# A decoder layer on one core: stick-breaking weights by a VectorE scan along the keys and TensorE transposes, tokens in reverse order, and banded attention's bias and row maximum in one VectorE instruction

## The chip, the cores and the metric

The kernel runs on one core of a Trainium2 chip. Time is device time in microseconds (us) of one execution of the whole program, and lower is better. The engines are named as in the profile: PE is TensorE (matrix products; PEld is its weight load, which overlaps), DVE is VectorE, ACT is ScalarE, POOL is GpSimd and SP is SyncE, which here only issues transfers. Three runs of the kernel before gave 802.22 to 802.78 us.

## The reference

One decoder layer on 512 tokens of width 1024, in float32. After an RMS norm, one wide projection feeds three mixers, each with its own sigmoid gate: banded attention (8 query heads, 2 key heads, window 128, a bias by distance, a sink), stick-breaking attention (8 heads of 64), and attention over 256 memory tokens (4 heads of 128). Then a projection, a second norm and a SwiGLU layer. The parts that the change touches:

```python
# stick-breaking, for every query t (rows) and key s (columns), z = q.k / 8
causal = key < query
log_1m  = where(causal, log_sigmoid(-z), 0)
between = reverse_cumsum(log_1m) - log_1m          # over keys between s and t
a       = where(causal, exp(log_sigmoid(z) + between), 0)
out     = a @ v
# banded attention, 128 queries against 256 keys
scores = where(in_window, scores + bias, -inf)
m = max(max(scores), sink);  p = exp(scores - m)
w = p / (sum(p) + exp(sink - m))
```

So the weight of key s is sigmoid(z) times the product of 1 - sigmoid(z) over the keys that lie between it and the query.

## The kernel before, in words

Everything is computed with tokens or features on the 128 partitions. A float32 product is made of three products of parts: `split` (L134) writes a rounded high part on ACT (L136) and the rest on DVE (L137), and `mm3` (L166) multiplies high by high, high by low and low by high (L168 to L170).

The work is laid out in one Python program, from which a scheduler makes the order on each engine: it goes by program order as priority, by when it expects an instruction's inputs to be there, and by the buffers that are free. `after` (L187) adds order edges that cost no wait. On the chip each engine then works through its list in order and waits where an input is late. Two helpers shape the program order:

- `Stream` (L33) holds the dense projections (weight load by SP, split, products) in a queue of units, and `run(us)` emits units worth about `us` of PE time. The attention code calls it between its own stages, so that PE has projections to work on while ACT and DVE prepare the next attention products. A generator `yield 7.0` in `sb_head` is such a request for 7.0 us.
- `table` (L199) loads an ACT function table and pins every later function call behind it; Exp and Ln share one table, Sigmoid has another.

`sb_head` (L838 on) runs once for each of 8 heads, in `SEG`ments of the causal triangle packed in three PSUM tiles of 512, 384 and 384 columns (the last one holds the two smallest blocks). Scores are transposed, keys on the partitions: eight products and three mask products into `z`. ACT and DVE form softplus(z) by Abs, Exp, Ln (L869 and the two calls after it) and a DVE combination (L872), which is then split into `sh` and `sl` (L877, L878). After the filler of 7.0 us PE adds the sum over keys into the same `z` by products with a triangle of -1 (`ntri_r`) and blocks of -1 (`none_r`, `none`), 14 records in all; ACT takes Exp, and the result is the weight tile that the value product `ysb` reads, once for every two heads.

`swa_pair` (L913) does banded attention for two heads at a time: scores with queries on the partitions, bias added on DVE (L933 to L935) into a tile whose unused first block POOL fills (L932), row maxima by `tensor_reduce` (L943), Exp on ACT with a running sum, a scaling on DVE (L955), seven transposes through PE (L966), copies, and the value product `ysw`.

[...] The gates of stick-breaking are projected between the heads; their Sigmoid runs in one block when all heads are done (`sigmoids`, L325), between two table loads. The values of both mixers lie in `v_all`, written at L347.

Of the kernel before, what the change touches and what calls it, by code (L numbers as in the profile page):

```python
# [10 lines left out]
F32 = mybir.dt.float32  # L11
# [94 lines left out]
def tile_kernel(ctx, tc, a):  # L106
# [251 lines left out]

    def vcols(t, lo):
        return v_all[:, t * 640 + lo : t * 640 + lo + 64]  # L360
# [24 lines left out]
    def mem_keys(i):  # L385
        def gen(hi, lo):
            if i % 2 == 0:
                st[("mk", i // 2)] = ck(f"mk{i}")
            t = st[("mk", i // 2)][:, (i % 2) * M : (i % 2 + 1) * M]
            ps = dps(f"pmk{i}")  # L390
            for k in range(KC):
                mm3(ps[:, :M], cols((hi, lo), k * P, P), mu[k], k == 0, k == KC - 1)
                yield 0.325
            nc.vector.tensor_tensor(t, ps[:, :M], st["mrb"][:, :], op=ALU.mult)
            if i % 2 == 1:
                st[("mks", i // 2)] = parts(f"mks{i // 2}", st[("mk", i // 2)])

        return gen

    def mem_vals(q):  # L400
        def gen(hi, lo):
            if q == 0:
                st["pmv"] = [dps(f"pmv{t}") for t in range(2)]
            for i in range(2):
                k = 2 * q + i
                for t in range(2):
                    x = (mu[k][0][:, t * P : (t + 1) * P], mu[k][1][:, t * P : (t + 1) * P])
                    mm3(st["pmv"][t][:, :], x, cols((hi, lo), i * 512, 512), k == 0, k == KC - 1)
                    yield 0.65
                    if k == KC - 1:  # L410
                        vt = ck(f"mv{t}")
                        nc.vector.tensor_scalar(
                            vt[:, :], st["pmv"][t][:, :], st["mrs"][:, t : t + 1], None, op0=ALU.mult
                        )
                        st[("mvs", t)] = parts(f"mvs{t}", vt)

        return gen
# [358 lines left out]
    ntri = const("ntri", [P, P])  # L776
# [5 lines left out]
    sinks = cst.tile([P, 8], F32, name="sinks")  # L782
    nc.sync.dma_start(sinks[:, :], a["sinks"].to_broadcast([P, 8]))
    ntri_r = cst.tile([P, P], F32R, name="ntri_r")
    nc.gpsimd.tensor_copy(ntri_r[:, :], ntri[:, :])
    none = cst.tile([P, P], F32, name="none")
    nc.gpsimd.memset(none[:, :], -1.0)
    nc.gpsimd.tensor_scalar(g_neg[:, :], g_pre, -1.0, None, op0=ALU.mult)
    none_r = cst.tile([P, P], F32R, name="none_r")
    nc.gpsimd.tensor_copy(none_r[:, :], none[:, :])  # L790

# [46 lines left out]
    def sb_head(h):  # L838
        c = h // 2
        ks, qs, ql = (st[(x, c, h % 2)] for x in ("kbs", "qbs", "qbl"))  # L840
        z = [aps(f"z{h}{i}") for i in range(3)]

        def seg(ts, j):
            i, o, n = SEG[j]
            return ts[i][:, o : o + n]

        for j in range(4):
            i, o, n = SEG[j]
            kj = slice(j * P, (j + 1) * P)
            if j < 3:  # L850
                out, qh, qlo = z[i][:, o : o + n], qs[:, j * P :], ql[:, j * P :]
            else:

                out = z[i][:, o : o + 2 * n]
                qh = qs[:, j * P :].unsqueeze(1).to_broadcast([P, 2, P])
                qlo = ql[:, j * P :].unsqueeze(1).to_broadcast([P, 2, P])
            mm(out, ks[:, kj], qh, j < 3, False)
            mm(out, ks[:, kj], qlo, False, False)

        for i in range(2):  # L860
            mm(z[i][:, :P], identb[:, :], negm[:, :], False, False)
        blocks23 = z[2][:, :].rearrange("p (b n) -> p b n", b=4)[:, 0:4:2, :]
        mm(blocks23, identb[:, :], negm[:, :].unsqueeze(1).to_broadcast([P, 2, P]), False, False)
        e = [ck(f"e{h}{i}") for i in range(3)]
        sh = [ck(f"sh{h}{i}", F32R) for i in range(3)]
        sl = [ck(f"sl{h}{i}", F32R) for i in range(3)]
        for i in range(3):
            x, n = e[i][:, : W[i]], W[i]
            nc.scalar.activation(x, z[i][:, :n], AF.Abs)  # L869
            fn(x, x, AF.Exp, scale=-1.0)  # L870
            st["chain"] = fn(x, x, AF.Ln, bias=1.0)
            nc.vector.scalar_tensor_tensor(x, z[i][:, :n], 0.0, x, op0=ALU.max, op1=ALU.add)  # L872
            if i == 2:

                nc.vector.tensor_tensor(e[i][:, 384:], e[i][:, 128:256], e[i][:, 256:384], op=ALU.add)
                x, n = e[i][:, :], 512
            nc.vector.tensor_copy(sh[i][:, :n], x)  # L877
            nc.vector.tensor_tensor(sl[i][:, :n], x, sh[i][:, :n].bitcast(F32), op=ALU.subtract)  # L878
        yield 7.0

        def both(t):

            return t[2][:, :].rearrange("p (b n) -> p b n", b=4)[:, 0:4:3, :]


        for j in range(3):
            for t in (sh, sl):
                mm(z[j][:, : W[j]], ntri_r[:, :], t[j][:, : W[j]], False, j == 2 and t is sl)
        for t in (sh, sl):
            mm(z[0][:, 128:], none_r[:, :], seg(t, 1), False, False)  # L890
        for t in (sh, sl):
            mm(z[0][:, 256:], none_r[:, :], both(t), False, t is sl)
            mm(z[1][:, 128:384], none_r[:, :], both(t), False, t is sl)
        mm(z[2][:, 128:256], none[:, :], seg(e, 3), False, True)
        for i in range(3):
            fn(e[i][:, : W[i]], z[i][:, : W[i]], AF.Exp)
        yield 3.0 if h % 2 == 0 else 4.0
        if h % 2 == 0:
            st["even"] = e
            return  # L900


        ys = aps(f"ysb{c}")
        for j in (3, 2, 1, 0):
            for i, x in ((1, e), (0, st["even"])):
                mm(ys[64 * i : 64 * i + 64, j * P :], vcols(j, 128 + (2 * c + i) * 64), seg(x, j), j == 3, j == 0)
        pair_out(SB, c, ys)


    def blocks(t, n):  # L910
        return t[n // 2][:, (n % 2) * 256 : (n % 2) * 256 + 256]

    def swa_pair(c, bias):  # L913
        hs = (c, c + 4)
        s, w, pt, pts = {}, {}, {}, {}
        for i, h in enumerate(hs):
            qs, ks, kl = st[("qas", c, i)], st[("kas", 0, i)], st[("kal", 0, i)]
            s[h] = [aps(f"s{h}{i}") for i in range(2)]
            for n in (1, 0, 2, 3):
                q = slice(n * P, (n + 1) * P)  # L920
                if n == 0:
                    kh = ks[:, :P].unsqueeze(1).to_broadcast([P, 2, P])
                    klo = kl[:, :P].unsqueeze(1).to_broadcast([P, 2, P])
                else:
                    keys = slice((n - 1) * P, (n + 1) * P)
                    kh, klo = ks[:, keys], kl[:, keys]
                mm(blocks(s[h], n), qs[:, q], kh, n in (1, 2), False)
                mm(blocks(s[h], n), qs[:, q], klo, False, True)
        for h in hs:
            b = bias[h // 2][:, (h % 2) * 256 : (h % 2) * 256 + 256]  # L930
            w[h] = [ck(f"w{h}{i}") for i in range(2)]
            nc.gpsimd.memset(w[h][0][:, :P], NEG)  # L932
            nc.vector.tensor_tensor(w[h][0][:, P:256], s[h][0][:, P:256], b[:, P:256], op=ALU.add)  # L933
            nc.vector.tensor_tensor(w[h][0][:, 256:], s[h][0][:, 256:], b, op=ALU.add)
            nc.vector.tensor_tensor(  # L935
                w[h][1][:, :].rearrange("p (n k) -> p n k", n=2),
                s[h][1][:, :].rearrange("p (n k) -> p n k", n=2),
                b.unsqueeze(1).to_broadcast([P, 2, 256]),
                op=ALU.add,
            )  # L940
            nm, den, es = (small(f"{x}{h}") for x in ("nm", "den", "es"))
            for i in range(2):
                nc.vector.tensor_reduce(  # L943
                    nm[:, 2 * i : 2 * i + 2], w[h][i][:, :].rearrange("p (n k) -> p n k", n=2), axis=AX.X, op=ALU.max
                )
            nc.vector.tensor_scalar(nm, nm, sinks[:, h : h + 1], -1.0, op0=ALU.max, op1=ALU.mult)
            fn(es, nm, AF.Exp, bias=sinks[:, h : h + 1])
            for n in range(NT):
                x = blocks(w[h], n)
# [3 lines left out]
            for n in range(NT):  # L953
                x = blocks(w[h], n)
                nc.vector.tensor_scalar(x, x, den[:, n : n + 1], None, op0=ALU.mult)  # L955
        yield 10.0
        for h in hs:

            pt[h] = [aps(f"pt{h}{i}") for i in range(2)]
            for n in range(NT):  # L960
                for e in range(2):
                    j = n - 1 + e
                    if j < 0:
                        continue
# [3 lines left out]
            nc.scalar.copy(pts[h][0][:, :], pt[h][0][:, :])  # L968
            nc.vector.tensor_copy(pts[h][1][:, :384], pt[h][1][:, :384])
        yield 2.0  # L970
        ys = aps(f"ysw{c}")
        for j in range(NT):
            n = 256 if j < 3 else P
            for i, h in enumerate(hs):
                mm(ys[64 * i : 64 * i + 64, j * P : j * P + n], vcols(j, i * 64), blocks(pts[h], j)[:, :n], j == 0, j == 3)
# [43 lines left out]
    bias = band_bias()  # L1019
    for h in range(8):  # L1020
# [4 lines left out]
    table("sigmoid_and_others")  # L1025
    sigmoids(SB)
# [544 lines left out]
def _constants():  # L1571
# [3 lines left out]
    for k in range(128):  # L1575
        oh[b[k], 255 - k] = 1.0
    wm = np.full((P, 384), NEG, np.float32)
    wm[:, 128:256] = 0.0
    return {
        "ident": np.eye(P, dtype=np.float32),  # L1580
        "ntri": -(i[:, None] >= i[None, :]).astype(np.float32),
# [6 lines left out]
def _layout(i):  # L1588
# [5 lines left out]
    x, mem = i["x"][0], i["mem"][0]  # L1594
# [60 lines left out]
```

## Time and profile before

| What | Value |
|---|---|
| median of 3 runs | 802.58 us |
| profiled execution, first to last instruction | 801.9 us |
| PE / DVE / ACT / POOL busy | 791.9 / 608.0 / 474.8 / 105.2 us |
| granted PE clock | 0.998 |
| DMA | 123.43 MB, mean 154 GB/s |
| stick-breaking heads | about 80 to 213 us |
| banded attention | about 215 to 290 us |

A row of groups in the profile gives line, engine, operation, written and read tiles, shape, count, then busy time in total, mean duration of one in ns, and the engine's idle time before them with what ended it. A row of the timeline gives start, length, engine, line, operation, tiles, shape and count. PE records overlap (the next one starts before the modelled end of the last one), so a PE instruction's price is the distance from its start to the start of the next one, not its duration.

### The profile page before, as it was taken

The page shows a single profiled execution, that of the slowest core. Times are in us where ns is not written, and L with a number is a line of the kernel's source. Part 1 is how long each engine was busy: PE and PEld are TensorE (multiplying, and loading weights), DVE is VectorE, ACT ScalarE, POOL GpSimd, SP SyncE. Part 2 cuts the span into 40 slices and gives each one's busy share as a digit, 9 for nine tenths or more (in the row PEclk, how much of TensorE's full clock was granted, in tenths as well). Part 3 has the DMA queues.
Part 4 walks back from the last instruction along what each step waited for, and adds up shares of the span by engine and source line. Part 5 has one row for each costly group of instructions (what it writes and reads, how often), then busy time and mean ns, then how long its engine had stood idle before and what let it go on. Part 6 is the DMA issues. An engine that isn't in the chain of part 4 may idle for free.

```text
span 801.9 us, 12466 instructions
## 1 busy us (share of the span) xinstructions
PE 791.9 (99%) x4694; PEld 695.8 (87%) x4694; DVE 608.0 (76%) x957; ACT 474.8 (59%) x847; POOL 105.2 (13%) x131
## 2 busy tenths in 40 slices
PE   9999999999999999999999999999999999999996
PEld 6899888778788888888888899999999999888785
DVE  6895878656578876766876679867676777898797
ACT  7562766546776587557823466655544444666573
POOL 1203300000020120002062100100100000215200
PEclk9999999999999999999999999999999999999999
DMA  8444535221572478339869707987777762949802
GB/s 298 134 133 124 202 106 148 64 74 57 171 167 58 79 137 212 73 77 242 290 203 289 133 5 184 266 237 184 184 182 184 183 158 64 220 106 241 182 0 105
DMA packets 42876, 123.43 MB, mean 154 GB/s; under 512 B 5056, under 2 KB 6768, under 8 KB 42816
## 3 DMA queue, kind: packets, MB, share of 16 engines
q1 hardware_dynamic: 30912, 86.32, 33.6%
q0 software_dynamic: 11472, 35.93, 24.3%
q8 instruction: 36, 0.59, 0.3%
q10 hardware_dynamic: 432, 0.39, 0.1%
q14 instruction: 24, 0.20, 0.1%
HBM read 116.85 MB, written 3.67 MB: 150 GB/s over the span
## 4 chain that ended last, share of the span: by engine, by line
PE 88%; DVE 5%; DMA 3%; issue 2%; ACT 1%; POOL 1%; DVEq 0%; POOLq 0%; ACTq 0%
PE gx L168 5%; PE gx L170 5%; PE gx L169 5%; PE z L180 4%; DMA bp<-in_w_dn 3%; PE gy L170 3%; PE gy L168 3%; PE gy L169 3%; PE br L168 3%; PE br L169 3%; PE br L170 3%; PE mx L170 2%; PE mx L169 2%; PE mx L168 2%; PE g L168 2%
## 5 line engine op out<-in xcount | busy, mean ns | idle before, releaser
L136 ACT CAST hi<-gw 128x1024 fp32r<-128x1024 f32 x77 | 79.9, 1048 | 83.5 <-DVE gw L1231 39.9
L137 DVE TENSOR_TENSOR lo<-gw,hi 128x1024 fp32r<-128x1024 f32 x77 | 93.8, 1227 | 32.4 <-ACT hi L136 32.4
L137 DVE TENSOR_TENSOR lo<-raw,hi 128x1024 fp32r<-128x1024 f32 (+2 forms) x76 | 91.8, 1208 | 33.8 <-ACT hi L136 33.4
L136 ACT CAST hi<-raw 128x1024 fp32r<-128x1024 f32 (+2 forms) x76 | 78.4, 1037 | 44.7 <-PE pv L170 10.7
L1213 POOL DMA_DIRECT2D gw<-in_w_gu x27 | 23.3, 920 | 196.5 <-DMA gw<-in_w_gu 71.4
L136 ACT CAST hi<-r 128x1024 fp32r<-128x1024 f32 (+1 forms) x24 | 23.5, 981 | 19.8 <-PE y L170 5.3
L168 PE MATMUL x<-hi,lh 128*128 128x512 f32 x88 | 34.4, 390 | 0.3 <-ACT lh L136 0.3
L169 PE MATMUL x<-lo,lh 128*128 128x512 f32 x88 | 34.3, 389 | 0.0
L170 PE MATMUL x<-hi,ll 128*128 128x512 f32 x88 | 34.2, 390 | 0.0
L137 DVE TENSOR_TENSOR lo<-r,hi 128x1024 fp32r<-128x1024 f32 (+1 forms) x24 | 27.2, 1132 | 3.6 <-ACT hi L136 3.5
L137 DVE TENSOR_TENSOR lo<-bp,hi 128x512 fp32r<-128x512 f32 x33 | 22.7, 719 | 7.0 <-ACT hi L136 6.8
L456 POOL DMA_DIRECT2D raw<-in_w_g x16 | 13.9, 868 | 106.7 <-DVE lo L137 92.9
L193 ACT ACTIVATE e<-e 128x384 f32<-128x384 f32 (+1 forms) x48 | 26.9, 561 | 1.5
L136 ACT CAST hi<-bp 128x512 fp32r<-128x512 f32 x33 | 19.4, 620 | 14.1 <-DMA bp<-in_w_dn 5.0
L872 DVE SCALAR_TENSOR_TENSOR e<-z,e 128x384 f32<-128x384 f32 (+1 forms) x24 | 14.3, 597 | 15.7 <-ACT e L193 15.7
L168 PE MATMUL g<-uh,hi 128*128 128x512 f32 x64 | 25.4, 398 | 0.0
L170 PE MATMUL g<-uh,lo 128*128 128x512 f32 x64 | 25.3, 396 | 0.0
L168 PE MATMUL gx<-B11h,hi 128*128 128x256 f32 x88 | 25.1, 285 | 0.2 <-ACT B11h L1142 0.2
L168 PE MATMUL gx<-T4h,hi 128*128 128x256 f32 x88 | 25.1, 285 | 0.0
L169 PE MATMUL g<-ul,hi 128*128 128x512 f32 x64 | 25.0, 391 | 0.0
L170 PE MATMUL gy<-N22h,lo 128*128 128x256 f32 x88 | 25.0, 284 | 0.0
L168 PE MATMUL gy<-N22h,hi 128*128 128x256 f32 x88 | 25.0, 284 | 0.0
(792 smaller groups left out, 2831.5 us busy)
## 6 DMA issues: line engine op xcount, KB each, us to landing
gw<-in_w_gu SPq DMA_DIRECT2D x57, 512.0 KB, 4.9
gw<-in_w_gu POOLq DMA_DIRECT2D x27, 512.0 KB, 7.3
raw<-in_w_p SPq DMA_DIRECT2D x22, 512.0 KB, 3.7
raw<-in_w_g POOLq DMA_DIRECT2D x16, 512.0 KB, 6.1
raw<-in_w_g SPq DMA_DIRECT2D x12, 512.0 KB, 3.6
bp<-in_w_dn SPq DMA_DIRECT2D x22, 256.0 KB, 11.2
r<-in_w_dn POOLq DMA_DIRECT2D x10, 512.0 KB, 9.2
raw<-in_w_brt SPq DMA_DIRECT2D x8, 512.0 KB, 4.4
```

The lines of the kernel that those rows point to most:

```text
L136: ins = nc.scalar.copy(hi, raw)
L137: lows = nc.vector.tensor_tensor(lo, raw, hi.bitcast(F32), op=ALU.subtract)
L168: one = nc.tensor.matmul(out, lh, rh, start=start, stop=False, skip_group_check=True)
L169: nc.tensor.matmul(out, lh, rl, start=False, stop=False, skip_group_check=True)
L170: return one, nc.tensor.matmul(out, ll, rh, start=False, stop=stop, skip_group_check=True)
L180: return nc.tensor.matmul(out, l, r, start=start, stop=stop, skip_group_check=True)
L193: ins = nc.scalar.activation(*args, **kw)
L456: nc.gpsimd.dma_start(t[:, :], src, accum_op=ALU.add)
L872: nc.vector.scalar_tensor_tensor(x, z[i][:, :n], 0.0, x, op0=ALU.max, op1=ALU.add)
L1213: nc.gpsimd.dma_start(gw[(n, key)][:, :], g_src(n, i, j), accum_op=ALU.add)
```

## The change

Stick-breaking now has queries on the partitions and keys along the columns, and the host hands over the tokens in reverse, so that the keys behind a query stand to its right, nearest first. ACT writes sigmoid(z) and sigmoid(-z); a DVE scan along the columns computes state = (1 - b)·state + b, the running sum of the weights. The tile is then turned by ten PE transposes of 128 x 128 a head, copied out of PSUM by ACT, and multiplied with differences of neighbouring values instead of the values (summation by parts). For these, eight transfers on SP copy `v_all` shifted by one token, and four DVE subtractions follow the first head's scans. The three triangle and block products and their splits are gone.

Because the heads now use Sigmoid, the table is switched before the heads, once the memory's norm (`mrs`) is there, and the gates' Sigmoids run one by one as each gate is projected. Banded attention uses one `tensor_tensor_reduce` for each block (bias added, maximum with the sink folded in) in place of add, fill and reduce, with the band on the right side, and ACT and DVE swap their two copies. Two evacuations of the memory keys and values get high priority, and some constants go.

```diff
+    def next_values():
+        st["vnext"] = [ck(f"vnext{t}") for t in range(NT)]
+        for t, x in enumerate(st["vnext"]):
+            if t == NT - 1:
+                nc.vector.memset(x[96:, :], 0.0)
+            else:
+                nc.sync.dma_start(x[P - 1 :, :], own_values(t + 1)[:1, :])
+            nc.sync.dma_start(x[: P - 1, :], own_values(t)[1:, :])
+
+    def value_steps():
+        for t, x in enumerate(st.pop("vnext")):
+            after(nc.vector.tensor_tensor(own_values(t), own_values(t), x[:, :], op=ALU.subtract), st["scan"])
...
-            nc.vector.tensor_tensor(t, ps[:, :M], st["mrb"][:, :], op=ALU.mult)
+            with tc.high_priority():
+                nc.vector.tensor_tensor(t, ps[:, :M], st["mrb"][:, :], op=ALU.mult)
...
-            mm(out, ks[:, kj], qh, j < 3, False)
-            mm(out, ks[:, kj], qlo, False, False)
+            mm(out, qs[:, q], keys, r < 3, False)
+            mm(out, ql[:, q], keys, False, False)
...
+        w = [ck(f"bw{h}{i}") for i in range(3)]
+        rest = [ck(f"br{h}{i}") for i in range(3)]
         for i in range(3):
-            x, n = e[i][:, : W[i]], W[i]
-            nc.scalar.activation(x, z[i][:, :n], AF.Abs)
-            fn(x, x, AF.Exp, scale=-1.0)
-            st["chain"] = fn(x, x, AF.Ln, bias=1.0)
-            nc.vector.scalar_tensor_tensor(x, z[i][:, :n], 0.0, x, op0=ALU.max, op1=ALU.add)
-            if i == 2:
-                nc.vector.tensor_tensor(e[i][:, 384:], e[i][:, 128:256], e[i][:, 256:384], op=ALU.add)
-                x, n = e[i][:, :], 512
-            nc.vector.tensor_copy(sh[i][:, :n], x)
-            nc.vector.tensor_tensor(sl[i][:, :n], x, sh[i][:, :n].bitcast(F32), op=ALU.subtract)
-        yield 7.0
+            n = W[i]
+            fn(rest[i][:, :n], z[i][:, :n], AF.Sigmoid, scale=-1.0)
+            st["chain"] = fn(w[i][:, :n], z[i][:, :n], AF.Sigmoid)
+        for i, o, n in SEG:
+            x, r = w[i][:, o : o + n], rest[i][:, o : o + n]
+            st["scan"] = nc.vector.tensor_tensor_scan(x, r, x, 0.0, op0=ALU.mult, op1=ALU.add)
+        yield 7.5
...
-        for j in range(3):
-            for t in (sh, sl):
-                mm(z[j][:, : W[j]], ntri_r[:, :], t[j][:, : W[j]], False, j == 2 and t is sl)
-        for t in (sh, sl):
-            mm(z[0][:, 128:], none_r[:, :], seg(t, 1), False, False)
-        for t in (sh, sl):
-            mm(z[0][:, 256:], none_r[:, :], both(t), False, t is sl)
-            mm(z[1][:, 128:384], none_r[:, :], both(t), False, t is sl)
-        mm(z[2][:, 128:256], none[:, :], seg(e, 3), False, True)
-        for i in range(3):
-            fn(e[i][:, : W[i]], z[i][:, : W[i]], AF.Exp)
+        pt = [aps(f"zt{h}{i}") for i in range(3)]
+        at = [ck(f"at{h}{i}") for i in range(3)]
+        KEY = [(2, 256), (2, 0), (1, 0), (0, 0)]
+        for r in range(NT):
+            i, o, _ = SEG[r]
+            for j in range(r, NT):
+                t, base_col = KEY[j]
+                nc.tensor.transpose(
                    pt[t][:, base_col + r * P : base_col + (r + 1) * P],
                    w[i][:, o + (j - r) * P : o + (j - r + 1) * P],
                    ident[:, :],
                )
+        nc.scalar.copy(at[0][:, :], pt[0][:, :])
+        nc.scalar.copy(at[1][:, :384], pt[1][:, :384])
+        nc.scalar.copy(at[2][:, :384], pt[2][:, :384])
         yield 3.0 if h % 2 == 0 else 4.0
...
-            nc.gpsimd.memset(w[h][0][:, :P], NEG)
-            nc.vector.tensor_tensor(w[h][0][:, P:256], s[h][0][:, P:256], b[:, P:256], op=ALU.add)
...
+            for n in range(NT):
+                nc.vector.tensor_tensor_reduce(
+                    band(w[h], n), band(s[h], n), b[:, : BAND[n]],
+                    scale=1.0, scalar=sink, op0=ALU.add, op1=ALU.max, accum_out=nm[:, n : n + 1],
+                )
...
     bias = band_bias()
+    next_values()
+    while "mrs" not in st:
+        dn.piece()
+    table("sigmoid_and_others")
+    sigmoids(SB)
     for h in range(8):
         for us in sb_head(h):
             dn.run(us)
     st.pop("chain")
     dn.until(f"gates{SB}")
-    table("sigmoid_and_others")
-    sigmoids(SB)
     table("natural_log_exp_and_others")
...
-    x, mem = i["x"][0], i["mem"][0]
+    x, mem = i["x"][0][::-1], i["mem"][0]
```

More of the change, by code (lines that the diff above doesn't have):

```diff
@@ L911, in blocks, with band @@
         return t[n // 2][:, (n % 2) * 256 : (n % 2) * 256 + 256]
+    BAND = (256, 256, 256, P)
+    def band(t, n):
+        return blocks(t, n)[:, : BAND[n]]
     def swa_pair(c, bias):
@@ L931, in swa_pair @@
             w[h] = [ck(f"w{h}{i}") for i in range(2)]
[L932 to L940, printed above, removed]
-            nm, den, es = (small(f"{x}{h}") for x in ("nm", "den", "es"))
-            for i in range(2):
-                nc.vector.tensor_reduce(
-                    nm[:, 2 * i : 2 * i + 2], w[h][i][:, :].rearrange("p (n k) -> p n k", n=2), axis=AX.X, op=ALU.max
-                )
-            nc.vector.tensor_scalar(nm, nm, sinks[:, h : h + 1], -1.0, op0=ALU.max, op1=ALU.mult)
-            fn(es, nm, AF.Exp, bias=sinks[:, h : h + 1])
+            nm, den, es = (small(f"{x}{h}") for x in ("nm", "den", "es"))
+            sink = sinks[:, h : h + 1]
+            for n in range(NT):
+                nc.vector.tensor_tensor_reduce(
+                    band(w[h], n),
+                    band(s[h], n),
+                    b[:, : BAND[n]],
+                    scale=1.0,
+                    scalar=sink,
+                    op0=ALU.add,
+                    op1=ALU.max,
+                    accum_out=nm[:, n : n + 1],
+                )
+            nc.vector.tensor_scalar(nm, nm, -1.0, None, op0=ALU.mult)
+            fn(es, nm, AF.Exp, bias=sink)
             for n in range(NT):
-                x = blocks(w[h], n)
+                x = band(w[h], n)
                 fn(x, x, AF.Exp, bias=nm[:, n : n + 1], accum_out=den[:, n : n + 1])
@@ L953, in swa_pair @@
             for n in range(NT):
-                x = blocks(w[h], n)
+                x = band(w[h], n)
                 nc.vector.tensor_scalar(x, x, den[:, n : n + 1], None, op0=ALU.mult)
@@ L967, in swa_pair @@
             pts[h] = [ck(f"pts{h}{i}") for i in range(2)]
-            nc.scalar.copy(pts[h][0][:, :], pt[h][0][:, :])
-            nc.vector.tensor_copy(pts[h][1][:, :384], pt[h][1][:, :384])
+            nc.vector.tensor_copy(pts[h][0][:, P:], pt[h][0][:, P:])
+            nc.scalar.copy(pts[h][1][:, :], pt[h][1][:, :])
         yield 2.0
         ys = aps(f"ysw{c}")
-        for j in range(NT):
-            n = 256 if j < 3 else P
+        for j in (3, 2, 1, 0):
+            q, o = ((j - 1) * P, 0) if j > 0 else (0, P)
             for i, h in enumerate(hs):
-                mm(ys[64 * i : 64 * i + 64, j * P : j * P + n], vcols(j, i * 64), blocks(pts[h], j)[:, :n], j == 0, j == 3)
+                mm(ys[64 * i : 64 * i + 64, q : (j + 1) * P], vcols(j, i * 64), blocks(pts[h], j)[:, o:], j == 3, j == 0)
         pair_out(SWA, c, ys)
```

83 lines of the change are left out of this document (37 added, 46 removed).

## The prediction, made before the change was run

> **What bounds the kernel now.** I read the page's engine shares first, then the waits of PE, then the busy time of each engine in the stages that the change touches.
>
> ```profile
> span 801.9 us, 12466 instructions
> PE 791.9 (99%) x4694; PEld 695.8 (87%) x4694; DVE 608.0 (76%) x957; ACT 474.8 (59%) x847; POOL 105.2 (13%) x131
> ```
> ```profile
> PE warm L180 <- DVE idle L728: 1.4, 1, 1.4
> PE z L180 <- DVE sl L878: 1.1, 1, 1.1
> ```
> ```profile
> 80.00:112.00 32.00, 32.00 (x189) 27.77 (x189) 26.23 (x44) 23.13 (x39) 6.07 (x9) 1.00 0.51 163
> 112.00:145.00 33.00, 33.00 (x190) 27.41 (x186) 24.93 (x39) 22.38 (x37) 0.00 (x0) 1.00 0.42 126
> 145.00:178.00 33.00, 31.94 (x164) 25.99 (x162) 19.90 (x33) 17.88 (x31) 0.00 (x0) 1.00 0.22 64
> 178.00:213.00 35.00, 35.00 (x177) 28.05 (x174) 18.49 (x30) 21.67 (x38) 0.00 (x0) 1.00 0.42 128
> 232.00:290.00 58.00, 57.91 (x330) 47.16 (x331) 49.83 (x108) 35.15 (x86) 8.16 (x14) 1.00 0.48 101
> ```
>
> The last fence has a window (us from the start), its length, then the busy time of PE, PEld, DVE, ACT and POOL (with counts), the granted clock, the DMA share and GB/s. The reader is to see three things. PE is at work 99% of the span, and its two longest waits are 1.4 us (the warm-up at the start) and 1.1 us (in the heads, for the last `sl`). In the four windows of the heads PE is full save for that wait, at a granted clock of 1.00, while DVE falls from 82% (26.23 of 32) to 53%, ACT stays at 54 to 72%, and the DMA share at or below 0.51. In banded attention (last window) PE is full too, but DVE is at 86%. So a microsecond of PE work taken out is a microsecond of time, as long as what DVE and ACT must deliver still comes before PE asks for it; a microsecond off DVE or ACT alone is worth nothing.
>
> **PE work removed.** The chain of work shows the sum over keys of one head in one piece, 14 records:
>
> ```profile
> 102.10 2.20 PE z L180 x14
> ```
>
> Eight heads: 8 x 2.20 = 17.6 us. The scores keep their eight products of the same widths (only the operands swap sides), the masks and the value product their counts; banded attention keeps 16 products and 14 transposes a pair. They cost nothing either way.
>
> **PE work added.** Ten transposes a head. The trace has 14 of the same shape in a row:
>
> ```profile
> 228.20 1.69 PE L966 MATMUL pt<-c_ident,w 128*128 128x128 f32 x14
> 229.65 0.47 PE L168 MATMUL qm<-uh,hi 128*128 128x512 f32 x1
> ```
>
> From the first one to the next product are 1.45 us, 0.104 us each; 80 of them are 8.3 us. PE's balance is -17.6 + 8.3 = -9.3 us. The 1.1 us wait is one for `sl`, which no longer exists: with it, -10.4 us, if nothing new is late.
>
> **What DVE and ACT must do for a head, and whether it is in time.** Rows of the heads' stage (the page's form, shapes apart):
>
> ```profile
> L878 DVE TENSOR_TENSOR sl<-e,sh 128x512 fp32r<-128x512 f32 x16 | 11.0, 688 | 0.3
> L872 DVE SCALAR_TENSOR_TENSOR e<-z,e 128x384 f32<-128x384 f32 x16 | 8.8, 550 | 0.0
> L877 DVE CAST sh<-e 128x512 fp32r<-128x512 f32 x16 | 7.1, 442 | 0.5
> L872 DVE SCALAR_TENSOR_TENSOR e<-z,e 128x512 f32<-128x512 f32 x8 | 5.5, 690 | 15.7 <-ACT e L193 15.7
> L878 DVE TENSOR_TENSOR sl<-e,sh 128x384 fp32r<-128x384 f32 x8 | 4.5, 559 | 0.3
> L877 DVE CAST sh<-e 128x384 fp32r<-128x384 f32 x8 | 2.9, 360 | 0.3
> L875 DVE TENSOR_TENSOR e<-e 128x128 f32<-128x128 f32 x8 | 2.3, 292 | 0.3
> L193 ACT ACTIVATE e<-e 128x384 f32<-128x384 f32 x32 | 16.8, 526 | 1.0
> L193 ACT ACTIVATE e<-e 128x512 f32<-128x512 f32 x16 | 10.1, 632 | 0.5
> L869 ACT ACTIVATE e<-z 128x384 f32<-128x384 f32 x16 | 7.6, 474 | 0.0
> L193 ACT ACTIVATE e<-z 128x384 f32<-128x384 f32 x16 | 7.3, 490 | 0.0
> L193 ACT ACTIVATE e<-z 128x512 f32<-128x512 f32 x8 | 4.8, 600 | 22.5 <-PE z L180 20.8 <-DVE ka L299 1.7
> L869 ACT ACTIVATE e<-z 128x512 f32<-128x512 f32 x8 | 4.8, 598 | 9.4 <-PE z L180 9.4
> ```
> ```profile
> L596 POOL TENSOR_TENSOR gq2p<-gq2p,gq0p 128x512 f32<-128x512 f32 x6 | 8.5, 1413 | 31.3 <-DVE gq2p L593 31.3
> L137 DVE TENSOR_TENSOR lo<-raw,hi 128x1024 fp32r<-128x1024 f32 x21 | 25.6, 1219 | 2.4 <-ACT hi L136 2.4
> ```
> ```profile
> L933 DVE TENSOR_TENSOR w<-s,bias x8: 280/280/281, 216.2 to 273.5; 128x128 f32<-128x128 f32 x8
> L934 DVE TENSOR_TENSOR w<-s,bias x8: 412/416/419, 216.4 to 273.8; 128x256 f32<-128x256 f32 x8
> L935 DVE TENSOR_TENSOR w<-s,bias x8: 678/680/681, 216.7 to 274.1; 128x512 f32<-128x512 f32 x8
> ```
>
> DVE loses all seven rows: 42.1 us, 5.26 us a head. It gains four scans of 512, 384, 256 and 128 columns. No row shows a scan. Lower bound, as one plain pass each: 0.69 + 0.55 + 0.42 + 0.29 = 1.95 us a head. Upper bound, by the slowest elementwise row (POOL's 1413 ns for 512, 2.76 ns a column): 1280 columns, 3.5 us. I take the upper one, since a scan feeds each column into the next. Even so DVE is relieved by 1.7 us a head. ACT loses 51.4 us, 6.43 a head; it gains six functions out of PSUM, 2 x (0.60 + 0.49 + 0.49) = 3.16 us, and three copies that I price like L869 (0.60 + 2 x 0.47 = 1.55): relieved by 1.7 us.
>
> The latency is what counts. The tightest head of before:
>
> ```profile
> 160.85 0.60 ACT L869 ACTIVATE e<-z 128x512 f32<-128x512 f32 x1 [0.68 <-PE z L180]
> 166.31 0.39 PE L180 MATMUL z<-sh,ntri_r 128*128 128x512 f32 x1
> 168.44 0.68 DVE L878 TENSOR_TENSOR sl<-e,sh 128x512 fp32r<-128x512 f32 x1
> 169.18 0.44 PE L180 MATMUL z<-sl,ntri_r 128*128 128x384 f32 x1 [1.06 <-DVE sl L878]
> ```
>
> ACT starts at 160.85, the last `sl` is there at 169.12 (8.3 us), PE comes at 166.31 (5.5 us) and waits 1.06 us for the last part. With the new chain the first pair of functions is done 1.2 us after ACT's start, at 162.05, the scans at 162.05 + 3.5 = 165.6, or 166.8 with one weight split (1219 ns) in between. PE would come 0.5 us later (7.5 for 7.0 asked), at 166.8, and needs the last block 0.7 us (seven transposes) later still. So the chain is shorter by 1.5 us or more and its turn comes later: no wait, cost 0, covered by the filler. If that cover went, each us late would cost 8 us over the heads.
>
> [...]
>
> **The rest of the change.** Value differences: four subtractions of 512 columns at 0.69 us = 2.8 us on DVE once, within the 5.8 us that DVE has free in the first window and the relief above; the first reader, `ysb`, stood at 110 us, 25 us after the first head's scans. Behind them in DVE's list stand weight splits, which PE has three units (about 15 us) ahead. The eight shifted transfers on SP wait for `v_all`, written by about 81 us; behind them stand weight loads, issued four units (about 20 us) ahead. Their price as transfers, and the table's:
>
> ```profile
> xq<-xq POOLq DMA_DIRECT2D x8, 256.0 KB, 4.8
> L201 ACT ACT_TABLE_LOAD  x8: 1283/1283/1283, 207.0 to 690.9; - x8
> L193 ACT ACTIVATE g<-g x8: 612/617/632, 209.3 to 216.3; 128x512 f32<-128x512 f32 x8
> L943 DVE TENSOR_REDUCE nm<-w 128x2 f32<-128x512 f32 x16 | 10.2, 676 | 1.2 <-POOL w L932 1.2
> ```
>
> About 4.8 us each and all eight in flight together: 0 on the path (bounds 0 and 5, if the weight loads behind them came that much late once). The table load moves in front of the first head: Ln and Exp of the memory's norm, then 1.28 us, delay the first Sigmoid by about 2.5 us once; the filler covers it, or 2 us are lost (bounds 0 to 2; I take 0, since PE had nothing to wait for when the same norm ran inside the first head). The last gate's Sigmoid is asked for 2.0 us of filler after its projection, and by my count of the filler (2.6 + 88.0 against 88.4 + 2.0 and the next step) it is emitted only after the switch back to Exp and Ln; it may bring two more table loads (2.6 us of ACT). ACT has 23 us free in the window of banded attention: 0. The eight gate functions (0.62 us each) no longer stand in one block: 0, PE was full there.
>
> Banded attention, a head: DVE loses 0.28 + 0.42 + 0.68 + 2 x 0.68 = 2.74 us and gains three blocks of 256 and one of 128. Lower bound, the add alone: 3 x 0.42 + 0.28 = 1.54. Upper bound, add and reduce one after the other: twice that, 3.1. I take the middle, 2.3: DVE is relieved a little. At the upper end DVE has 0.35 us more a head, 2.8 us over 58 us, and stays under 92%. POOL's fill, the constants, the priorities of the memory evacuations and the swapped copies: 0 each, beside a full PE that did not wait for any of them.
>
> **Sum.** -17.6 + 8.3 - 1.1 = -10.4 us. The profiled execution's span is 801.9 us, 0.7 us under the median of the runs (802.58), the part outside first and last instruction, which I keep. 801.9 - 10.4 + 0.7 = 792.2 us.
>
> **Rivals.**
> 1. *The heads wait a little.* The scheduler orders by what it expects; a weight split of 1.22 us put in front of a head's last scan gives a wait like the one seen (1.06 us). In all eight heads that is 8.5 us: 800.7 us. For it: it happened once. Against: it happened once in eight, with a longer chain.
> 2. *The scan is slow: slower than before.* If scans take S us a head, PE waits S - (167.5 - 162.05 - 1.22) = S - 4.2. From S = 5.5 us (4.3 ns a column) the eight waits of 1.3 us eat the whole gain. At 8 ns a column, S = 10.2, each head waits 6.0 us, 48 us in all: 840 us. For it: no row shows a scan, and it is the one operation that must finish a column before the next. Against: the deciding 4.3 ns is 1.6 times the slowest elementwise row, 8 ns three times.
> 3. *Banded attention becomes DVE's.* If the fused instruction costs more than both old ones (say twice the upper bound's excess and its read-out, 1 us a head), DVE's 49.83 us in that stage become 57.8 of 58 and some 3 us are lost: 795 us. For it: DVE 86%. Against: two passes are already the upper bound.
> 4. *The removed work was hidden.* Then about 802.6 us. Against: PE has no wait to hide it behind.
>
> **Chances.** Forecast 0.64, rival 1 (between 795 and 801) 0.14, rival 2 0.11, rival 3 0.08, rival 4 0.03. A measurement of this kernel can tell about 0.2%, 1.6 us. Faster than 801.0: the forecast, rival 3 and most of rival 1, 0.83; within 0.2%: rival 4 and the rest of rival 1, 0.05; slower: 0.12. The range goes from 789.8 (other small waits gone as well) to 800.7 (rival 1 whole) and leaves out rivals 2 and 4.
>
> **What would show it.** After: PE busy near 782 us and still 98 to 99% of the span; no `ntri_r` or `none` rows, 80 transposes at about 0.10 us from start to start; the heads' stage some 10 us shorter; scan rows between 1.95 and 3.5 us a head; DVE busy 580 to 600 us, ACT near 461. Wrong: a PE wait for a scan or an `at` copy in several heads, PE idle before the first head's transposes behind the table load, or SP's weight loads behind the shifted transfers.

## The result and the profile after

| | before | after |
|---|---|---|
| median on the same chip | 802.52 us (4 runs, 802.22 to 802.78) | 834.1 us (4 runs, 832.75 to 835.13) |
| profiled execution, first to last instruction | 801.9 us | 830.9 us |
| PE / DVE / ACT busy | 791.9 / 608.0 / 474.8 us | 785.4 / 589.1 / 460.7 us |

Of the runs further down, one execution of 987.6 us at a granted clock of 0.75, against 0.98 in the three others of its program, is left out of the median.

The kernel is slower: the ratio is 1.0391, interval 1.0376 to 1.0406. The prediction was 792.2 us, so it is 42 us off and on the wrong side. Yet PE, DVE and ACT all became less busy, as predicted. The time was not spent, it was waited away. The page of the kernel after (span, busy time, the slices of PE and of its granted clock, and one group):

```profile
span 830.9 us, 12323 instructions
PE 785.4 (95%) x4662; PEld 689.0 (83%) x4662; DVE 589.1 (71%) x938; ACT 460.7 (55%) x825; POOL 102.8 (12%) x120
...
PE   9999823999999999999999999999999999999996
...
PEclk9999955999999999999999999999999999999999
...
L374 DVE TENSOR_TENSOR v_all<-v_all,vnext 128x512 f32<-128x512 f32 x4 | 2.8, 692 | 37.8 <-DMA vnext<-v_all 37.8
```

A slice is 20.8 us. Save for the last slice, where the kernel ends, PE is at 9 everywhere but in the fifth to seventh, that is from about 83 to 145 us, and in the last two of them its granted clock falls to a half as well. Nearly all that went wrong lies in these 62 us, in the middle of the heads. The last row names the suspect: DVE stood 37.8 us before the four value subtractions, for the shifted transfers. PE's waits in the kernel after (line that waits, what it waits for, total, times, longest):

```profile
PE pmk L168 <- DVE qa L299: 34.2, 2, 19.4
PE warm L180 <- DVE idle L747: 1.4, 1, 1.4
PE zt L890 <- DVE bw L880: 1.1, 2, 0.9
```

PE did not wait for the subtractions, whose result it needs late (its first product with the values, `ysb`, starts at 148.3 us), but for `qa`, evacuations of the query projection that free PSUM: the kernel gives `qa` and `pmk` one pool, `dps`, of two tiles. DVE's list in that time shows why (start, length, operation, idle time before it; other work of DVE stands between the last two rows):

```profile
101.73 0.69 DVE L374 TENSOR_TENSOR v_all<-v_all,vnext 128x512 f32<-128x512 f32 x1 [9.70 <-DMA vnext<-v_all]
112.23 0.69 DVE L374 TENSOR_TENSOR v_all<-v_all,vnext 128x512 f32<-128x512 f32 x1 [9.81 <-DMA vnext<-v_all]
112.84 1.22 DVE L137 TENSOR_TENSOR lo<-raw,hi 128x1024 fp32r<-128x1024 f32 x1
113.97 0.68 DVE L299 SCALAR_TENSOR_TENSOR qa<-qa,rb_x 128x512 f32<-128x512 f32 x1
122.70 0.69 DVE L374 TENSOR_TENSOR v_all<-v_all,vnext 128x512 f32<-128x512 f32 x1 [8.05 <-DMA vnext<-v_all]
133.61 0.69 DVE L374 TENSOR_TENSOR v_all<-v_all,vnext 128x512 f32<-128x512 f32 x1 [10.22 <-DMA vnext<-v_all]
...
137.76 0.66 DVE L299 SCALAR_TENSOR_TENSOR qa<-qa,rb_x 128x512 f32<-128x512 f32 x1
```

The four subtractions start 10.5, 10.5 and 10.9 us apart, each as one more transfer lands, and the evacuations stand between and behind them in DVE's list: PE is busy 0.00 us from 100 to 110 us and DVE 0.69, yet `qa` comes at 113.97, after DVE's wait of 9.81 us for the second transfer, and the last one at 137.76, after the fourth subtraction. 10.9 us for 127 rows is 86 ns a row. SP's queue and the windows of the stall (window, length, busy time of PE, PEld, DVE, ACT and POOL with counts, granted clock, DMA share, GB/s):

```profile
82.88 8.17 SPq L369 DMA_DIRECT2D vnext<-v_all  x1
91.09 0.63 SPq L370 DMA_DIRECT2D vnext<-v_all  x1
91.76 11.63 SPq L369 DMA_DIRECT2D vnext<-v_all  x1
103.43 10.28 SPq L370 DMA_DIRECT2D vnext<-v_all  x2
113.81 27.00 SPq L148 DMA_DIRECT2D raw<-in_w_mv  x3
```
```profile
100.00:110.00 10.00, 0.00 (x0) 0.00 (x0) 0.69 (x1) 0.00 (x0) 0.00 (x0) 0.70 0.08 25
110.00:120.00 10.00, 4.43 (x24) 4.22 (x24) 2.43 (x3) 4.90 (x9) 0.00 (x0) 0.62 0.07 25
120.00:130.00 10.00, 0.00 (x0) 0.00 (x0) 0.69 (x1) 0.00 (x0) 0.00 (x0) 0.55 0.39 122
130.00:135.00 5.00, 0.00 (x0) 0.00 (x0) 1.35 (x2) 0.00 (x0) 0.00 (x0) 0.50 0.06 25
135.00:140.00 5.00, 1.43 (x7) 1.46 (x8) 4.94 (x8) 1.49 (x3) 0.00 (x0) 0.50 0.01 3
```

From 100 to 120 us the core moves 25 GB/s with a DMA share of 0.07 to 0.08. One of 16 engines at work all the time is a share of 0.06. So it looks as if a transfer of 127 rows, 254 KB, goes through one DMA engine alone (254 KB in 10.9 us is 24 GB/s), four of them one after the other, while the other 15 engines have almost nothing to do; the experiments test this. SP's issue instructions are held up with them, three of the seven for 8 to 12 us each, and three of the four loads of `w_mv` are not issued until 113.81 us. The chain of work says the same in one line:

```profile
91.09 42.50 DMA vnext<-v_all x2
```

### The profile page after: what moved, and what is told of

Read it like the earlier page. It is cut to its first block, busy times and chain, and to the rows that moved or that the text cites. A ratio compares the mean times of both kernels' runs of the same rounds, so it can differ in the third digit from the quotient of the medians.

```text
span 830.9 us, 12323 instructions
## 1 busy us (share of the span) xinstructions
PE 785.4 (95%) x4662; PEld 689.0 (83%) x4662; DVE 589.1 (71%) x938; ACT 460.7 (55%) x825; POOL 102.8 (12%) x120
## 4 chain that ended last, share of the span: by engine, by line
PE 86%; DMA 7%; DVE 2%; issue 2%; SPq 1%; ACT 1%; DVEq 0%; POOL 0%; POOLq 0%
PE gx L168 5%; DMA vnext<-v_all 5%; PE gx L170 5%; PE gx L169 5%; PE gy L170 3%; PE gy L168 3%; PE br L168 3%; PE gy L169 3%; PE br L169 3%; PE br L170 3%; PE x L170 2%; PE x L168 2%; PE x L169 2%; PE g L170 2%; PE g L168 2%
## 5 line engine op out<-in xcount | busy, mean ns | idle before, releaser
L137 DVE TENSOR_TENSOR lo<-raw,hi 128x1024 fp32r<-128x1024 f32 (+2 forms) x76 | 91.8, 1208 | 38.2 <-ACT hi L136 37.8
L168 PE MATMUL pmk<-mh,hi 128*128 128x256 f32 x32 | 10.8, 338 | 34.2 <-DVE qa L299 34.2
L168 PEld LDWEIGHTS pmk<-mh,hi 128*128 128x128 f32 x32 | 7.4, 232 | 34.8 <-issue 19.6
L880 DVE TENSOR_TENSOR_SCAN bw<-br,bw 128x512 f32<-128x512 f32 (+3 forms) x32 | 24.3, 808 | 13.9 <-ACT bw L193 13.9
L170 PE MATMUL x<-hi,ll 128*128 128x512 f32 x88 | 34.2, 390 | 0.0
L374 DVE TENSOR_TENSOR v_all<-v_all,vnext 128x512 f32<-128x512 f32 x4 | 2.8, 692 | 37.8 <-DMA vnext<-v_all 37.8
L264 ACT CAST qas<-qa 64x512 fp32r<-64x512 f32 x8 | 4.9, 617 | 39.4 <-DVE qa L299 39.2
```

Source lines behind the costliest of these rows:

```text
L137: lows = nc.vector.tensor_tensor(lo, raw, hi.bitcast(F32), op=ALU.subtract)
L168: one = nc.tensor.matmul(out, lh, rh, start=start, stop=False, skip_group_check=True)
L170: return one, nc.tensor.matmul(out, ll, rh, start=False, stop=stop, skip_group_check=True)
L264: nc.scalar.copy(x[r : r + 64, :], t[r : r + 64, :])
L374: after(nc.vector.tensor_tensor(own_values(t), own_values(t), x[:, :], op=ALU.subtract), st["scan"])
L880: st["scan"] = nc.vector.tensor_tensor_scan(x, r, x, 0.0, op0=ALU.mult, op1=ALU.add)
```

## The experiments

The theories after this result. A: the number of rows, 127, puts each transfer on one DMA engine of SP's queue, and the order of DVE's and SP's lists turns that into PE's wait. B: SBUF-to-SBUF copies of this size, or seven of them on SP, are slow or in the way however they are cut. A puts the run with 112 + 15 rows at 790 to 796 us, by the author's estimate that these counts go over several engines. Beside these stands the question what else is left between the prediction and a kernel without the stall.

**Cut each transfer into 112 + 15 rows.**

```diff
-            nc.sync.dma_start(x[: P - 1, :], own_values(t)[1:, :])
+            nc.sync.dma_start(x[:112, :], own_values(t)[1:113, :])
+            nc.sync.dma_start(x[112 : P - 1, :], own_values(t)[113:, :])
```

> The changed kernel with each transfer of 127 rows cut into one of 112 and one of 15 rows; nothing else. [...] Rival 1 (copies within SBUF that shift by a partition are slow whatever their count): the same bytes take as long, about 830 us. Rival 2 (the loss comes from the scans or the table switch): above 805 us.

Measured: 796.74 us (795.98 to 797.08), ratio 0.9918 (0.9903 to 0.9934). The same bytes by the same queue, with four transfers more, and 37 us are gone; the kernel is now 0.8% faster than the one before, and 0.7 us above the upper end of theory A's range. How many engines 112 or 15 rows go over is not shown. Its page, four of its larger PE waits with the one for `qa`, and the shifted tile's rows (DVE's wait for it, then the time from issue to landing):

```profile
span 795.3 us, 12326 instructions
PE 782.8 (98%) x4662; PEld 686.5 (86%) x4662; DVE 589.0 (74%) x938; ACT 460.7 (58%) x825; POOL 102.7 (13%) x120
```
```profile
PE g2p L168 <- ACT gq2p L564: 1.3, 2, 1.0
PE zt L891 <- DVE bw L881: 1.1, 2, 0.9
PE br L168 <- DVE qm L299: 0.7, 1, 0.7
PE pmv L168 <- DVE mk L413: 0.5, 1, 0.5
...
PE pmk L168 <- DVE qa L299: 0.3, 1, 0.3
```
```profile
  DMA vnext<-v_all: 2.6, 1
...
DMA to landing us min/median/max: 1.7/4.6/7.5
```

The spans differ by 35.6 us, and this adds up: the wait for `qa` falls from 34.2 to 0.3 us (33.9), PE's busy time from 785.4 to 782.8 (2.6: products between and behind the two waits ran at a granted clock of 0.62 to 0.50), and one other wait, for `gq2p`, grows by 0.9.

**Cut into 113 + 14 rows instead.** 113 is a prime like 127.

> The changed kernel with each transfer of 127 rows cut into one of 113 rows (a prime number) and one of 14; the same number of transfers and bytes as in the cut at 112. Theory (row count decides the number of DMA engines): 113 rows stay on one engine, 113 x 86 ns = 9.7 us each, so the time stays near 825 us (815 to 832). Rival 3 (it is the size or number of transfers, not the divisor): like the cut at 112, near 792 us.

Measured: 828.7 us in one run. The number and the sizes of the transfers are as above to within one row, and the stall is back. Its PE wait, then the shifted tile's rows:

```profile
PE pmk L168 <- DVE qa L299: 29.3, 2, 16.4
```
```profile
L375 DVE TENSOR_TENSOR v_all<-v_all,vnext x4: 691/691/692, 101.0 to 129.8; 128x512 f32<-128x512 f32 x4
...
  DMA vnext<-v_all: 33.8, 4
```

DVE again waits 33.8 us for the four, and between the first and the last subtraction lie 28.8 us, 9.6 for each transfer or 85 ns a row of 113, the pace of the 127 rows (86 ns). From 100 to 120 us the DMA share is 0.08 to 0.09, at 27 to 28 GB/s, about one engine of 16 again. So the number of rows decides, and not the size of the pieces; that it does so by its divisors was the author's estimate and is not shown. That settles A against B as far as the row count goes. Beside the small rests, only row counts of 127, 113 and 112 were run.

**Leave the values out.** No shifted transfers and no subtractions.

```diff
-            if h == 0:
-                value_steps()
...
-    next_values()
```

> The changed kernel without the shifted transfers and without the four subtractions: the values are used as they are, so the stick-breaking output is not the reference's. It gives the price of everything else in the change. Theory: 792 us (790 to 795), PE waits for nothing longer than about 1 us in the heads. Rival 2 (scans, turns or table switch cost time too): 797 us or more.

Measured: 795.36 us (794.5 to 795.69), ratio 0.9899 (0.988 to 0.9919), span 793.8. That lies between the two ranges given above. So all that the values cost in the 112 + 15 form is about 1.5 us, and what remains above 792.2 is not theirs.

**The transfers on POOL's queue.** 127 rows as in the change.

```diff
-                nc.sync.dma_start(x[P - 1 :, :], own_values(t + 1)[:1, :])
-            nc.sync.dma_start(x[: P - 1, :], own_values(t)[1:, :])
+                nc.gpsimd.dma_start(x[P - 1 :, :], own_values(t + 1)[:1, :])
+            nc.gpsimd.dma_start(x[: P - 1, :], own_values(t)[1:, :])
```

> The changed kernel with the seven shifted transfers issued from POOL in place of SP; still 127 rows, still subtracted on DVE. SP's weight loads no longer stand behind them. Theory (DVE waits in its list for 4 x 10.9 us of one engine's work): no gain, 822 to 832 us. If SP's queue was the harm: 796 to 800 us. If POOL's queue spreads 127 rows over all engines: 796 us as well, and the packets' rows will show it (many engines, not one).

Measured: 801.9 us (800.65 to 803.43), ratio 0.9982 (0.9972 to 0.9992). The shifted tile's rows (the last line is the time from issue to landing):

```profile
L370 POOL DMA_DIRECT2D vnext<-v_all x4: 536/541/564, 91.8 to 95.6; - x4
...
  DMA vnext<-v_all: 6.9, 2
...
DMA to landing us min/median/max: 4.8/6.7/7.0
```

Neither outcome came: the 822 to 832 us of the theory were wrong, since on this queue the seven transfers land in 4.8 to 7.0 us, 6.7 in the median, where one of 127 rows took 10.5 to 10.9 us on SP's, and 796 us was not reached. How many engines they go over is not shown. The price in the prediction, 4.8 us, was read from a row of this queue and equals the lowest of these. What is left of the loss is, by the waits, place: POOL issues them at 91 to 96 us only, behind the transfers of the bias, so DVE waits 6.9 us and PE 4.4 us for `qa`.

**The same, ahead of the bias.** The calls `next_values()` and `band_bias()` change places.

> The shifted transfers of 127 rows on POOL's queue as in the earlier run, but laid out ahead of the bias work, so that they do not stand behind the bias's transfers (there they were issued at 91 us, 10 us after the values were ready, and DVE waited 6.9 us). On POOL's queue 127 rows landed in 6.7 us. Theory: DVE's wait falls below 2 us, and the time is near the cut kernel's: 796 to 799 us. If the queue itself is slow: 801 to 803 us as before.

Measured: 804.54 us (802.15 to 805.55), ratio 1.001 (0.9999 to 1.0022). A miss. The transfers are issued at 78 to 82 us and land in 4.1 to 7.1, as hoped, but POOL's list now stands 12.3 us for `v_all` to be written, and the bias, which came first before, comes late:

```profile
PE pbias L180 <- POOL rbh L821: 5.0, 1, 5.0
```

That wait, and 3.1 us more of PE busy time than in the 112 + 15 form (785.9 against 782.8; why is not shown), take the gain away. On POOL's queue neither of the two places tried does as well as SP with 112 + 15 rows.

**Is it DVE's wait, or the loads behind the transfers?** The change with its transfers of 127 rows, but without the subtractions:

```diff
-            after(nc.vector.tensor_tensor(own_values(t), own_values(t), x[:, :], op=ALU.subtract), st["scan"])
+            pass
```

> The changed kernel with the transfers of 127 rows, but without the four subtractions (the values are not differenced, so the stick-breaking output is not the reference's). It parts the two ways in which the slow transfers can hurt. If DVE's list is what stands (subtractions in front of projections' evacuations and weight splits), the loss is gone: 792 to 796 us. If SP's weight loads behind the transfers are what is late, most of it stays: SP got the second half of the memory weights out only from 113.8 us on in the changed kernel, against a need at about 115 us; then 805 to 825 us, with PE waiting for weight splits. I expect something between, 793 to 810 us, since the loads are issued four units (about 20 us) ahead and the queue stands for 43 us.

Measured: 827.23 us (826.98 to 827.84), ratio 1.03 (1.0284 to 1.0317). It lies above both ranges and does not tell: with nobody to read the shifted tiles, their buffers were given out again, and ACT had to wait until the transfers into them had landed, 32.3 us in all: 22.5 before Sigmoids (`bw` here and 9.9 us before `br`) and 9.8 before a copy of `qa`.

```profile
ACT bw L193 <- DMA vnext<-v_all: 12.6, 2, 9.2
```

So the tiles were held by small POOL copies, laid out in the program behind the fifth head's scans. On the chip POOL made them as the transfers landed; in the first run's trace it waited for these 35.1 us in all, four times:

```diff
-            after(nc.vector.tensor_tensor(own_values(t), own_values(t), x[:, :], op=ALU.subtract), st["scan"])
+            after(nc.gpsimd.tensor_copy(x[:, :8], x[:, 8:16]), st["scan"])
...
-            if h == 0:
+            if h == 4:
```

> The changed kernel with its transfers of 127 rows on SP and without the subtractions (so the stick-breaking output is not the reference's), as in the run of transfers only; but the four shifted tiles stay occupied until a small POOL copy behind the fifth head's scans. In the run of transfers only, the scheduler gave their buffers to the second head's Sigmoid outputs, and ACT waited 32 us there for the slow transfers to land, so that run did not part the two ways. Theory A (DVE's wait is the only harm in the changed kernel; SP's late weight loads are hidden): 795 to 800 us. Theory B (the loads behind the transfers are harm enough): the three loads of memory weights land at about 126 to 134 us, the second of them is split by ACT for use at about 120 us, so PE loses some 10 to 20 us: 805 to 818 us. I lean to B.

Measured: 824.53 us in the median of three (824.01 to 825.21), ratio 1.0261 (1.0239 to 1.0283), above the range of theory B as well. The trace is that of a second run of the same program:

> The same program as the run with the shifted tiles held behind the fifth head (127 rows on SP, no subtractions, so the stick-breaking output is not the reference's); its three undisturbed executions took 824 to 825 us, but the profiled one was at a clock of 0.75. This run is for the profile. Theory B (SP's weight loads behind the transfers): 824 us again, PE's wait of some 20 to 30 us ends on ACT, and ACT's list stands at a weight split that waits for a load landing after 125 us. If ACT or DVE wait for the shifted tiles' buffers instead, the run does not part the two ways.

Measured: 824.43 us (823.83 to 825.04), ratio 1.0261 (1.024 to 1.0281). Without any wait on DVE for the transfers, 29 us more than without the transfers (1.0261 against 0.9899 of some 803). ACT's timeline, SP's, and PE's longest wait:

```profile
136.25 1.04 ACT L136 CAST hi<-raw 128x1024 fp32r<-128x1024 f32 x1 [31.98 <-DMA raw<-in_w_mv]
137.20 0.58 ACT L895 COPY at<-zt 128x512 f32<-128x512 f32 x1
```
```profile
114.29 11.63 SPq L148 DMA_DIRECT2D raw<-in_w_mv  x3
```
```profile
PE ysb L180 <- ACT at L895: 26.4, 1, 26.4
```

ACT's list stood 32 us at a weight split whose load lay behind the transfers, and the copies that PE needed for its value product stood behind that split. So the loads behind the transfers are harm enough by themselves, more than expected. In the kernel after DVE's wait lies over theirs and costs some 10 us more (834.1 against 824.43). By this, moving the subtractions down DVE's list alone would repair about 10 us at most; that was not run.

**What else keeps it above 792.2.** First the two extra table loads, on top of the 112 + 15 form: the last gate's Sigmoid is drained before the table is switched back.

```diff
+    while dn.deferred:
+        dn.piece()
```

> The kernel with transfers cut into 112 and 15 rows, and the stream run until the last gate's Sigmoid has been emitted before the switch back to Exp and Ln: two table loads (2.6 us of ACT) go. Theory (hidden, PE is full there): 796 to 797 us, same. If ACT's 2.6 us shows in PE's waits: 794 to 795 us.

Measured: 795.77 us (794.97 to 796.5), ratio 0.9899 (0.9878 to 0.992), span 794.4. ACT is busy 458.1 us instead of 460.7, so the two loads are gone; the span is 0.9 us less. The time lies between the two ranges, and the runs alone cannot tell it from nothing.

Then one more microsecond of filler for each head before its transposes (`yield 7.5` to `yield 8.5`), on top of that:

> The kernel with the cut transfers and the last gate's Sigmoid before the table switch, with 8.5 us of filler asked for in place of 7.5 between a head's scores and its turn. In the cut kernel the fourth head's scores stood only 3 us ahead of its turn, and PE waited 1.1 us for its scans (1.7 us with what the wait drew after it). Theory (the rest of the shortfall is the scan's latency in that one head): the wait goes, 793 to 795 us against 795.8. Otherwise the same, 795 to 797: the scheduler places the scores as before and the wait stays.

Measured: 800.24 us (799.12 to 801.81), ratio 0.9962 (0.9948 to 0.9975). A miss, above both ranges. The small wait for the scan is gone from PE's list, but the order of everything behind has changed, and two new waits stand there:

```profile
PE pt L976 <- ACT pts L979: 2.7, 1, 2.7
PE ysb L180 <- ACT at L896: 1.9, 1, 1.9
```

**Banded attention as before, within the new kernel.** The 112 + 15 form, with the fused instruction undone: three adds, three maxima and the sink.

```diff
-                nc.vector.tensor_tensor_reduce(
-                    band(w[h], n),
...
+            nc.vector.tensor_reduce(nm[:, :2], w[h][0][:, :].rearrange("p (n k) -> p n k", n=2), axis=AX.X, op=ALU.max)
+            nc.vector.tensor_reduce(nm[:, 2:3], w[h][1][:, :256], axis=AX.X, op=ALU.max)
+            nc.vector.tensor_reduce(nm[:, 3:4], w[h][1][:, 256:384], axis=AX.X, op=ALU.max)
+            nc.vector.tensor_scalar(nm, nm, sink, -1.0, op0=ALU.max, op1=ALU.mult)
```

> The kernel with transfers cut into 112 and 15 rows, and banded attention's four fused instructions a head replaced by three additions, three reductions and the sink's maximum, as the kernel before had them. Fused, a head costs 3 x 0.48 + 0.35 + 4 x 0.08 = 2.1 us of DVE; plain about 2.75 us. Theory (DVE is not the bound there even at 86%): same as the cut kernel, 796 to 798 us. If banded attention is DVE's: 799 to 803 us.

Measured: 798.98 us (798.72 to 800.18), ratio 0.9945 (0.9927 to 0.9964), span 797.2 against 795.3. That is at the border of the two ranges. The fused instruction seems worth some 2 us where I had expected none, though the two intervals just overlap. DVE is 5.9 us busier without it (594.9 against 589.0). How that reaches PE is open: PE's listed waits do not grow, its busy time does.

## Why the prediction was wrong

**The step that failed** is the price of the value differences: "About 4.8 us each and all eight in flight together: 0 on the path (bounds 0 and 5, if the weight loads behind them came that much late once)". It took a row of POOL's queue, a 256 KB transfer of 128 rows that adds into its target, for transfers of 127 rows on SP's queue (four of these, with three of a single row: seven in all, not eight). What the runs showed in its place: 10.5 to 10.9 us each, one after the other, at some 24 GB/s, because of the row count (112 + 15 rows repair it, 113 + 14 do not). From the kernel after to the 112 + 15 form that is 834.1 to 796.74 us.

The two covers that the step named went with it. "Behind them in DVE's list stand weight splits, which PE has three units (about 15 us) ahead" missed what else stands there: `qa`, whose evacuation frees PSUM. And a cover of 15 to 20 us hides 4.8 us, not 42. The last clause of "What would show it", SP's weight loads behind the shifted transfers, did come. I had the mechanism as a sign of error and gave it neither a price from the right queue nor a chance. No rival held it: the one on the slow side was the scan.

**What held.** PE busy "near 782 us": 782.8 without the stall, so 9.1 us less against a balance of 9.3. The transposes, predicted at 0.104 us, in the chain of work of the kernel after:

```profile
143.00 1.09 PE zt L890 x10
```

That is 0.109 us each.

The scans and the fused instruction of the kernel after, shapes apart (count, total, mean ns, idle before):

```profile
L945 DVE CUSTOM_DVE_ANT_0 w<-s,bias,sinks 128x256 f32<-128x256 f32 x24 | 10.4, 479 | 1.0 <-DMA xq<-xq 1.0
L880 DVE TENSOR_TENSOR_SCAN bw<-br,bw 128x512 f32<-128x512 f32 x8 | 9.8, 1225 | 13.9 <-ACT bw L193 13.9
L880 DVE TENSOR_TENSOR_SCAN bw<-br,bw 128x384 f32<-128x384 f32 x8 | 7.5, 934 | 0.0
L880 DVE TENSOR_TENSOR_SCAN bw<-br,bw 128x256 f32<-128x256 f32 x8 | 5.4, 674 | 0.0
L880 DVE TENSOR_TENSOR_SCAN bw<-br,bw 128x128 f32<-128x128 f32 x8 | 3.2, 398 | 0.0
L945 DVE CUSTOM_DVE_ANT_0 w<-s,bias,sinks 128x128 f32<-128x128 f32 x8 | 2.8, 346 | 0.0
L945 DVE DVE_READ_ACCUMULATOR2_ANT nm<- 128x1 f32 x32 | 2.7, 83 | 0.0
```

A head's scans take 1.225 + 0.934 + 0.674 + 0.398 = 3.23 us, within 1.95 to 3.5 and near the upper end that I took: rival 2 is out. Banded attention is (10.4 + 2.8 + 2.7) / 8 = 2.0 us a head on DVE, for 2.3 taken, bounds 1.54 and 3.1: rival 3 is out. DVE 589.1 and ACT 460.7 us lie where they were put. The two extra table loads came; without them the span was 0.9 us shorter, which is not clear of noise, where the sum has 0.

**What remains of the sum.** In the 112 + 15 form the profiled span is 795.3 us, against 791.5 predicted, 3.8 too long. PE's busy time accounts for 0.2. The rest is idle time: 12.5 us (795.3 - 782.8) where before had 10.0, while the sum took the 1.1 us wait as gone. It came back as a wait for a scan of 1.1 us, 0.9 of it in one head: rival 1 at a small scale. PE's lists of waits account for the other 2.5 us: they add up to 5.8 us here and to 3.3 before, and what is new are the waits for `gq2p` (1.3), `qm` (0.7), `mk` (0.5) and `qa` (0.3), less one of 0.3 for `lh` that only the kernel before has. The sum has no term for such waits. Why they came is not shown. With the values left out the span falls by 1.5 us, without the two table loads by 0.9, and the attempt to buy back the scan wait with filler cost more than it could gain.

## What to carry to other kernels

Price a transfer by a row of the same queue and the same shape, and look at the number of rows: on SP's queue here 127 rows took 10.5 to 10.9 us a transfer and 113 rows 9.6, one after the other, and with 112 + 15 rows all that the values cost was about 1.5 us. When a cost of 0 rests on a cover, ask what happens if the transfer takes three times as long: here DVE's list, which stood 37.8 us, and SP's, where three loads were issued only from 113.81 us on, passed the delay on to work that has nothing to do with the transfer. A small wait that is left need not be worth a change of filler: here one microsecond more of it moved the order of all that follows, and the kernel became about 4.5 us slower.

## What the hardware showed unexpectedly

- The same 127 rows of 2 KB took 10.5 to 10.9 us each, one after the other, on SP's queue; on POOL's, the seven transfers landed 4.8 to 7.0 us after their issue, and 4.1 to 7.1 when laid out ahead of the bias.
- In the run with the tiles held, the loads queued behind such transfers came late: SP issued three of `w_mv` from 114.29 us on, the page's slice from 102.8 to 123.3 us shows 26 GB/s, and ACT waited 32.0 us for a load of `w_mv`, until 136.25 us.
- At the end of the stall PE's granted clock was 0.50, and the first products of `pmk` (256 columns) started 0.21 us apart, at full clock again 0.12 us: the two waits, 34.2 us together, cost another 2.6.
